# Reordering the first stage of a hybrid attention block: where the adaLN sums stand among the transposes of x

## The chip, the cores and the metric

One core of a Trainium2 chip runs the whole kernel. The metric is device time in microseconds, the median of several executions. The engines are TensorE (PE; its weight loads are listed apart as PEld), VectorE (DVE), ScalarE (ACT), GpSimd (POOL) and the queue of SyncE (SP), which issues all loads of this stage.

## The reference, cut to what matters

The block works on x (1024 tokens by 1024 channels, float32). The part that the change touches is its beginning:

```python
ada = c @ w_ada[l] + b_ada[l]
shift, scale, gate = jnp.split(ada, 3, axis=-1)
h = rms_norm(x, norm_w[l]) * (1.0 + scale[:, None, :]) + shift[:, None, :]
proj = h @ w_in[l]
(cq, ckv, k_rope, gate_a, q_b, k_b, v_b, f_b, gate_b, mg_a, mg_b) = jnp.split(proj, split_points, axis=-1)
```

After it come two attention branches, gates, and the output projection, in which this change does nothing.

## The kernel before, in words

x is cut into eight tiles of 128 rows (x0 to x7). `phase0` (from L246) turns them into h, channel by row, and multiplies h with the first columns of `w_in` (`w_cq`, 424 columns: the query latent, the rope key and the forget gate). Channels are cut into eight blocks of 128 (kt 0 to 7).

For each x tile ScalarE squares it and sums each row (`square`, L271; a second small instruction reads the sum). For each pair of tiles `scale` (L274 to L286) takes the root on ScalarE, polishes its reciprocal on VectorE in four small steps and multiplies both tiles (L286). TensorE transposes a scaled tile with eight transposes against the identity (`turn`, L136) into two PSUM banks, four channel blocks each. `evac` (L307 to L311) copies the two halves into `xT`. Before, ScalarE copies both.

For each channel block the adaLN shift and scale are a matrix product of c with a block of `w_ada` (two tiles of 512 KB). For blocks 0 and 1 TensorE does it (`ada_rows`, L313 to L320: two halves, shift and scale, of eight float32 matmuls, each of which the trace lists as two instructions). For blocks 2 to 7 VectorE does it in two sums of 128x1024 (`ada_cols`, L322 to L324) with `cb`, c in every row. `gain` (L326 to L329) makes of them the two columns `gs`.

Then h is split into a rounded part and a rest so that float32 accuracy comes out of three fast products: `high` (L335, ScalarE) writes the high part `hT_hi`, `modulate` (L340 on ScalarE or L342 on VectorE) overwrites `xT` with h, `low` (L347, VectorE) writes the difference `hT_lo`. `w_cq` is split in the same way (cast on ScalarE, difference on VectorE). `products` runs the three products of a channel block for a list of row tiles: part 0 is high by high, part 1 high by low weights, part 2 low by high; 24 matmuls for a block of all eight tiles.

The order is written out by hand: each engine executes its instructions in the order of the lines, and waits for the operands of the one at its head. Before, TensorE's order is 32 warm transposes of the identity, x0 and x1, x2 and x3, both halves of block 0's sums, x4 and x5, products of block 0 for rows 0 to 3, both halves of block 1's sums, x6, products for rows 4 and 5, x7, products of block 1 for rows 0 to 5, then both blocks for rows 6 and 7, then blocks 2 to 7. SP issues the loads in the order of the lines too; a load waits for the landing of the load eight places before it.

PSUM tags: `s` has two slots of two banks, `t` two of one, `o` and `f` one each. A tile of a tag waits until the readers of the slot's last tile are through. Later stages are interleaved by a planner (`fill_to`, L142) that counts TensorE's time in `pe_time`; a warm transpose adds 107 ns to it (L135). All its due times are set from `pe_time` itself, as in

```python
self.fill_to(self.pe_time + 600)
due = self.pe_time
```

Of the kernel before, what the change touches and what calls it, by code (L numbers as in the profile page):

```python
# [10 lines left out]
F32 = mybir.dt.float32  # L11
F32R = mybir.dt.float32r
# [3 lines left out]
ALU = mybir.AluOpType  # L16
# [3 lines left out]
P = 128  # L20
# [54 lines left out]
class Net:  # L75
# [78 lines left out]
    def consts(self):  # L154
        nc, t, U = self.nc, self.t, self.U
        cp = self.cp
        self.x0 = U.get([P, D], F32, "x0")
        nc.sync.dma_start(self.x0, t["x"][0:P, :])
        self.ident = cp.tile([P, P], F32, name="ident")
        nc.sync.dma_start(self.ident, t["ident"])  # L160
        self.vec = cp.tile([P, t["vec"].shape[1]], F32, name="vec")
        nc.sync.dma_start(self.vec, t["vec"])
        self.misc_raw = self.Hs.get([P, 512], F32, "misc")
        self.pos = cp.tile([P, ST], I32, name="pos")
        self.ones = cp.tile([P, 1], F32, name="ones")
        nc.gpsimd.memset(self.ones, 1.0)
        self.eps = cp.tile([P, 1], F32, name="eps")
        nc.gpsimd.memset(self.eps, EPS)
        v = self.vec
        self.c_col = v[:, 0:8]  # L170
        self.nw = v[:, 8:16]
        self.b_shift = v[:, 16:24]
        self.b_scale = v[:, 24:32]
        self.lq = v[:, 32:35]
        self.lkv = v[:, 35:37]
        self.vqa_raw = v[:, 37:38]
        self.vka = v[:, 38:39]
        self.vqb_raw = v[:, 39:40]
        self.vkb = v[:, 40:41]
        self.bf_row = v[:, 41:49]  # L180
        self.b_gate = v[:, 49:57]
        self.b1 = cp.tile([P, KT], F32, name="b1")
        nc.vector.tensor_scalar(out=self.b1, in0=self.b_scale, scalar1=1.0, scalar2=None, op0=ALU.add)
        self.vqa = cp.tile([P, 1], F32, name="vqa")
        nc.vector.tensor_scalar(out=self.vqa, in0=self.vqa_raw, scalar1=float(96.0 ** -0.5), scalar2=None, op0=ALU.mult)
        self.vqb = cp.tile([P, 1], F32, name="vqb")
        nc.vector.tensor_scalar(out=self.vqb, in0=self.vqb_raw, scalar1=0.125, scalar2=None, op0=ALU.mult)
        self.maskb = cp.tile([P, P], BF16, name="maskb")
# [52 lines left out]
    def phase0(self):  # L241
# [11 lines left out]
        def load_x(*sts):  # L253
            for st in sts:
                xs[st] = U.get([P, D], F32, f"x{st}")
                nc.sync.dma_start(xs[st], t["x"][st * P:(st + 1) * P, :])

        def load(kt):
            wada[kt] = [U.get([P, D], F32, f"wada{kt}{e}") for e in range(2)]
            for e in range(2):  # L260
                nc.sync.dma_start(wada[kt][e], t["w_ada"][kt][:, e])

        def load_cq(gi, half=None):
            if not half:
                cqw.append(U.get([P, 2, 424], F32, f"raw_cq{gi}"))
            k = slice(0, 2) if half is None else slice(half, half + 1)
            nc.sync.dma_start(cqw[gi][:, k], t["w_cq"][:, 2 * gi + k.start:2 * gi + k.stop])

        def square(st):
            junk = Hs.get([P, 512], F32, f"junk{st}")  # L270
            nc.scalar.activation(junk.bitcast(BF16), xs[st], AF.Square, accum_out=ssq[:, st:st + 1])  # L271
            Hs.put(junk)

        def scale(pair):  # L274

            a, b = pair
            v, y, q = (self.sp.tile([P, 32], F32, tag=f"rs_{n}", name=f"{n}_x{a}", bufs=2)[:, 0:2] for n in "vya")
            nc.vector.tensor_scalar(out=v, in0=ssq[:, a:b + 1], scalar1=1.0 / D, scalar2=EPS, op0=ALU.mult, op1=ALU.add)
            nc.scalar.activation(y, ssq[:, a:b + 1], AF.Sqrt, scale=1.0 / D, bias=self.eps)
            nc.vector.reciprocal(y, y)  # L280
            nc.vector.scalar_tensor_tensor(out=q, in0=y, scalar=-0.5, in1=y, op0=ALU.mult, op1=ALU.mult)
            nc.vector.tensor_tensor(out=q, in0=q, in1=v, op=ALU.mult)
            nc.vector.scalar_tensor_tensor(out=y, in0=q, scalar=1.5, in1=y, op0=ALU.add, op1=ALU.mult)
            r = y
            for i, st in enumerate(pair):
                nc.vector.tensor_scalar(out=xs[st], in0=xs[st], scalar1=r[:, i:i + 1], scalar2=None, op0=ALU.mult)  # L286

        def warm(n, src):

            for _ in range(n):  # L290
                self.transpose(self.warm_bank[:, 0:P], src[:, 0:P])
# [18 lines left out]
                src = pts[st][j].rearrange("p (k c) -> p k c", k=4)  # L310
                (nc.scalar.copy if e == "a" else nc.vector.tensor_copy)(xT[:, 4 * j:4 * j + 4, cols], src)  # L311

        def ada_rows(kt, bank):  # L313

            b = self.bank(bank, f"pada{kt}")
            for e in range(2):
                w = wada[kt][e].rearrange("p (r c) -> p r c", r=8)
                for rc in range(8):
                    self.mm(b[:, 64 * e:64 * e + 64], w[:, rc], col(rc).broadcast_to([P, 64]), rc == 0, rc == 7)
            return b[:, 0:1], b[:, 64:65]  # L320

        def ada_cols(kt, e):  # L322
            w, a = wada[kt][e], acc[:, kt, e:e + 1]
# [9 lines left out]
        def high(kt, sts=range(ST)):  # L333
            c = slice(sts[0] * P, (sts[-1] + 1) * P)
            nc.scalar.activation(hi[:, kt, c], xT[:, kt, c], AF.Identity, scale=gs[:, kt, 1:2], bias=gs[:, kt, 0:1])  # L335
# [23 lines left out]

        self.wg = {}  # L360
        self.gcol = self.sp.tile([P, 8], F32, name="gcol")
        load_x(1, 2, 3, 4, 5)
        load(0)
        load_x(6, 7)
        load_cq(0, 0)
        load(1)
        load_cq(0, 1)
        self.cb = U.get([P, D], F32, "cb")
        nc.sync.dma_start(self.cb, t["c_row"].broadcast_to([P, D]))
        load_cq(1)  # L370
        most, last = range(6), (6, 7)
        self.warm_bank = self.bank("f", "warm")
        root = self.sp.tile([P, 1], F32, name="root")
        nc.scalar.activation(root, self.eps, AF.Sqrt)
        for st in range(4):
            square(st)
            if st % 2:
                scale((st - 1, st))
        warm(32, self.ident)
        turn(0, "s")  # L380
        turn(1, "tt")
        evac(0)
        square(4)
        evac(1)
        square(5)
        scale((4, 5))
        turn(2, "s")
        turn(3, "tt")
        evac(2)
        rows = ada_rows(0, "o")  # L390
        evac(3)
        gain(0, rows)
        square(6)
        high(0, range(4))
        wh, wl = U.get([P, 2, 424], F32R, "hi_cq0"), U.get([P, 2, 424], F32R, "lo_cq0")
        nc.scalar.copy(wh[:, 0], cqw[0][:, 0])
        turn(4, "tt")
        turn(5, "of")
        load(2)
        load(3)  # L400
        modulate(0, range(4), "d")
        low(0, range(4))
        evac(4)
        square(7)
        scale((6, 7))
        nc.vector.tensor_tensor(out=wl[:, 0], in0=cqw[0][:, 0], in1=wh[:, 0].bitcast(F32), op=ALU.subtract)
        self.cqw.append((wh, wl))
        evac(5)
        high(0, (4, 5))
        accs = [self.bank("s", f"cq_s{i}") for i in range(2)]  # L410
        for st in range(4):
            banks[st] = accs[st // 2][:, st % 2 * 512:st % 2 * 512 + 512]
        products(0, range(4), (0, 2))
        rows = ada_rows(1, "t")
        modulate(0, (4, 5), "d")
        low(0, (4, 5))
        gain(1, rows)
        nc.scalar.copy(wh[:, 1], cqw[0][:, 1])
        products(0, range(4), (1, ))
        load_cq(2)  # L420
        load(4)
        nc.sync.dma_start(self.misc_raw[:, 0:t["misc"].shape[1]], t["misc"])
        nc.sync.dma_start(self.pos, t["pos"])
        turn(6, "tt")
        high(1, most)
        modulate(1, most, "d")
        evac(6)
        low(1, most)
        banks[4], banks[5] = self.bank("o", "cq_o"), self.bank("f", "cq_f")
        products(0, (4, 5))  # L430
        turn(7, "tt")
        evac(7)
        nc.vector.tensor_tensor(out=wl[:, 1], in0=cqw[0][:, 1], in1=wh[:, 1].bitcast(F32), op=ALU.subtract)
        U.put(cqw[0])
        products(1, most, (0, 2, 1))
        wh, wl = U.get([P, 2, 424], F32R, "hi_cq1"), U.get([P, 2, 424], F32R, "lo_cq1")
        ada_cols(2, 0)
        ada_cols(2, 1)
        gain(2)
        load(5)  # L440
        banks[6], banks[7] = self.bank("t", "cq_t0"), self.bank("t", "cq_t1")
        for kt in range(2):
            high(kt, last)
            modulate(kt, last, "a")
        nc.scalar.copy(wh, cqw[1])
        for kt in range(2):
            low(kt, last)
        for kt in range(2):
            products(kt, last)
        high(2)  # L450
        modulate(2, engine="a")
        nc.vector.tensor_tensor(out=wl, in0=cqw[1], in1=wh.bitcast(F32), op=ALU.subtract)
# [995 lines left out]
def layout(i):  # L1448
# [21 lines left out]
    vec[0:64, 40] = vec[64:, 40] = a["kn_b"][0]  # L1470
    vec[:, 41:49] = a["b_f"][0][None, :]
    vec[:, 49:57] = b[2048:].reshape(8, P).T
    o["vec"] = vec
    o["c_row"] = np.ascontiguousarray(a["c"][0].reshape(1, D))
    o["pos"] = np.ascontiguousarray(a["positions"][0].reshape(8, P).T)
    inv = np.power(np.float32(10000), -np.arange(0, 32, 2, dtype=f) / np.float32(32)).astype(f)
# [3 lines left out]
    misc[:, 48:80] = a["kn_rope_a"][0]  # L1480
    misc[:, 80:208] = np.where(np.tril(np.ones((P, P), bool)), f(0), f(NEG))
    o["misc"] = misc
    o["ident"] = np.eye(P, dtype=f)
    r = np.arange(64)
    o["tri"] = ((r[:, None] // 8 == r[None, :] // 8) & (r[:, None] % 8 < r[None, :] % 8)).astype(f)
    o["w_cq"] = _chunks(np.concatenate([w_in[:, 0:384], w_in[:, 640:672], w_in[:, 2720:2728]], 1), 8)
# [31 lines left out]
```

## Time and profile before

| | us |
|---|---|
| median of 3 runs | 962.1 (961.2 to 963.23) |
| profiled execution, its own time | 961.75 |
| its span, first to last instruction | 959.9 |
| TensorE busy in the span | 947.9 (99%) |
| VectorE busy | 633.2 (66%) |
| ScalarE busy | 477.3 (50%) |
| GpSimd busy | 208.1 (22%) |

Times in the rows are microseconds from the start of the span, unless ns is said. The stage in question is the first 63 us. L numbers are lines of the kernel; L127 and L136 are the helpers through which all matmuls and transposes go, so there the tile names tell the groups apart.

### The profile page before, as it was taken

Reading aid. Unit: us, or ns where it says so; the run is one execution under the profiler, and the core shown is the slowest. Engines: PE = TensorE matmul, PEld = TensorE weight load, DVE = VectorE, ACT = ScalarE, POOL = GpSimd, SP = SyncE. Lnnn points to the kernel's source line nnn. Section 1 sums busy time; section 2 is a strip of 40 time slices with the busy share of each in tenths; the row PEclk is TensorE's granted clock in tenths of the full one; section 3 lists DMA queues with packets and bytes.
Section 4 is the critical chain, followed back from the end, with each engine's and each line's share of the span. In section 5 each row is a group of like instructions: output and inputs, shape, how many; then the busy total and the mean of one; then the engine's idle time right before and its main releaser. Section 6 shows DMA issues by size and latency. Waiting matters only on the chain.

```text
span 959.9 us, 14942 instructions
## 1 busy us (share of the span) xinstructions
PE 947.9 (99%) x5390; PEld 820.6 (85%) x5390; DVE 633.2 (66%) x1379; ACT 477.3 (50%) x959; POOL 208.1 (22%) x260
## 2 busy tenths in 40 slices
PE   7999999999999999999999999999999999999998
PEld 7999999998878888888888888888888888888887
DVE  3977877778366667657667676667676766495222
ACT  7776624543245556556555566465565654143000
POOL 0022142200012222221233333232333220046000
PEclk9999999999999999999999999999999999999999
DMA  9831132951973225235332232222421554644321
GB/s 340 334 98 45 51 114 62 323 216 40 343 232 110 88 67 132 71 95 133 99 91 68 66 101 89 80 88 89 120 70 46 186 186 154 238 147 138 103 88 66
DMA packets 79961, 124.96 MB, mean 130 GB/s; under 512 B 5928, under 2 KB 47536, under 8 KB 79888
## 3 DMA queue, kind: packets, MB, share of 16 engines
q1 hardware_dynamic: 79888, 124.01, 39.4%
q8 instruction: 42, 0.69, 0.3%
q14 instruction: 31, 0.25, 0.1%
HBM read 88.33 MB, written 35.66 MB: 129 GB/s over the span
## 4 chain that ended last, share of the span: by engine, by line
PE 92%; DMA 3%; DVE 2%; ACT 2%; issue 1%; SPq 1%; POOL 0%; ACTq 0%; DVEq 0%; POOLq 0%
PE f L127 36%; PE out L127 9%; PE s L127 9%; PE b L127 8%; PE o L127 7%; PE pt L136 6%; PE q L127 3%; PE ckv L127 2%; PE kv L127 2%; PE cq_s L127 2%; PE bv L127 1%; PE cq_t L127 1%; DMA x_u<-in_x 1%; PE pada L127 1%; DMA va_d<-vhl_u 1%
## 5 line engine op out<-in xcount | busy, mean ns | idle before, releaser
L1207 ACT CAST pp_u<-pt 128x512 fp32r<-128x512 f32 x192 | 91.9, 479 | 171.1 <-PE pt L136 155.0
L1208 DVE TENSOR_TENSOR pp_u<-pt,pp_u 128x512 fp32r<-128x512 f32 x192 | 106.7, 556 | 84.8 <-ACT pp_u L1207 81.9
L127 PE MATMUL f<-hT_lo,hi_f_u 128*128 128x512 f32 x384 | 153.6, 400 | 0.0
L127 PE MATMUL f<-hT_hi,lo_f_u 128*128 128x512 f32 x384 | 153.4, 399 | 0.0
L127 PE MATMUL f<-hT_hi,hi_f_u 128*128 128x512 f32 x384 | 153.1, 399 | 0.0
L127 PE MATMUL s<-k_u,q_u 96*128 96x512 f32 (+6 forms) x480 | 116.8, 362 | 0.9 <-DMA k_u<-kr_d 0.9
L1181 DVE TENSOR_REDUCE nm<-s 128x1 f32<-128x128 f32 (+7 forms) x128 | 97.0, 758 | 4.4
L1191 POOL TENSOR_SCALAR p_u<-p_u,rs 128x640 f32<-128x640 f32 (+1 forms) x64 | 64.3, 1004 | 164.1 <-DVE rs L1190 119.0
L1191 POOL TENSOR_SCALAR p_h<-p_h,rs 128x128 f32<-128x128 f32 (+1 forms) x64 | 41.7, 652 | 247.3 <-DVE rs L1190 208.2
L127 PE MATMUL o<-pp_u,v_u 128*128 128x512 f32 (+7 forms) x384 | 94.2, 340 | 0.0
L127 PEld LDWEIGHTS s<-k_u,q_u 96*128 96x128 f32 (+2 forms) x480 | 77.0, 190 | 7.3 <-issue 0.9
L127 PEld LDWEIGHTS f<-hT_hi,hi_f_u 128*128 128x128 f32 x384 | 72.4, 189 | 12.1
L127 PEld LDWEIGHTS f<-hT_hi,lo_f_u 128*128 128x128 f32 x384 | 72.4, 189 | 11.2
L127 PEld LDWEIGHTS f<-hT_lo,hi_f_u 128*128 128x128 f32 x384 | 72.5, 189 | 11.1
L127 PEld LDWEIGHTS o<-pp_u,v_u 128*128 128x128 f32 (+1 forms) x384 | 61.8, 161 | 19.5
L127 PE MATMUL b<-hi_b_u,hT_hi 128*128 128x256 f32 x256 | 73.1, 285 | 0.0
L127 PE MATMUL b<-hi_b_u,hT_lo 128*128 128x256 f32 x256 | 72.4, 283 | 0.0
L127 PE MATMUL b<-lo_b_u,hT_hi 128*128 128x256 f32 x256 | 72.4, 283 | 0.0
L136 PEld LDWEIGHTS pt<-ident,p_u 128*128 128x128 f32 x416 | 52.7, 140 | 16.7
L136 PE MATMUL pt<-ident,p_u 128*128 128x128 f32 x416 | 66.2, 272 | 0.0
L1187 ACT ACTIVATE p_u<-s,nm 128x640 f32<-128x640 f32 (+1 forms) x64 | 61.5, 961 | 4.3 <-DVE nm L1181 3.2
L127 PE MATMUL out<-lo_wo_u,hT_hi 128*128 128x512 f32 (+1 forms) x136 | 51.2, 377 | 0.0
(318 smaller groups left out, 2073.1 us busy)
## 6 DMA issues: line engine op xcount, KB each, us to landing
raw_f_u<-in_w_t SPq DMA_DIRECT2D x24, 512.0 KB
wada_u<-in_w_ada SPq DMA_DIRECT2D x16, 512.0 KB
mg_d<-th_h SPq DMA_DIRECT2D x32, 256.0 KB
mg_h<-mg_d SPq DMA_DIRECT2D x32, 256.0 KB
x_u<-in_x SPq DMA_DIRECT2D x8, 512.0 KB
raw_b_u<-in_w_b SPq DMA_DIRECT2D x8, 512.0 KB
raw_wg_u<-in_w_gate SPq DMA_DIRECT2D x8, 512.0 KB
va_d<-vhl_u SPq DMA_DIRECT2D x8, 512.0 KB
```

What stands on the lines that cost most here:

```text
L127: self.nc.tensor.matmul(out, lhsT=l, rhs=r, start=start, stop=stop)
L136: self.nc.tensor.transpose(out=out, in_=in_, identity=self.ident)
L1181: nc.vector.tensor_reduce(out=nm, in_=sv, axis=AX.X, op=ALU.max, negate=True)
L1187: nc.scalar.activation(p[:, 0:w], sv, AF.Exp, bias=nm, accum_out=sm)
L1191: nc.gpsimd.tensor_scalar(out=p[:, 0:w], in0=p[:, 0:w], scalar1=rs, scalar2=0.0, op0=ALU.mult, op1=ALU.add)
L1207: nc.scalar.copy(ph[:, c0:], pt[:, c0:])
L1208: nc.vector.tensor_tensor(out=pl[:, c0:], in0=pt[:, c0:], in1=ph[:, c0:].bitcast(F32), op=ALU.subtract)
```

## The change

Identity and constant vectors become one tensor with one load. The loads' order becomes x0, constants, x1, block 0 of `w_ada`, x2, x3, block 1, x4, x5, the first half block of `w_cq`, x6, x7, the second half block. `ada_rows` becomes `ada_row`, one half of a block's sum at a time. Evacuations are "ad": ScalarE copies channel blocks 0 to 3 of a tile, VectorE 4 to 7. TensorE's order becomes 24 warm transposes, the first half sum of block 0, x0, x1, its second half, x2, x3, both halves of block 1, products of block 0 for rows 0 to 3, x4, x5, products of block 1 for rows 0 to 3, x6, x7, products of both blocks for rows 4 to 7, then blocks 2 to 7 as before.

```diff
-        self.ident = cp.tile([P, P], F32, name="ident")
-        nc.sync.dma_start(self.ident, t["ident"])
-        self.vec = cp.tile([P, t["vec"].shape[1]], F32, name="vec")
-        nc.sync.dma_start(self.vec, t["vec"])
+        both = cp.tile([P, t["vec"].shape[1]], F32, name="vec")
+        nc.sync.dma_start(both, t["vec"])
+        self.ident, self.vec = both[:, 0:P], both[:, P:]
...
+        def ada_row(kt, e, bank):
+
+            w = wada[kt][e].rearrange("p (r c) -> p r c", r=8)
+            for rc in range(8):
+                self.mm(bank[:, 64 * e:64 * e + 64], w[:, rc], col(rc).broadcast_to([P, 64]), rc == 0, rc == 7)
+            return bank[:, 64 * e:64 * e + 1]
...
-        load_x(1, 2, 3, 4, 5)
+        load_x(1)
         load(0)
+        load_x(2, 3)
+        load(1)
+        load_x(4, 5)
+        load_cq(0, 0)
         load_x(6, 7)
-        load_cq(0, 0)
-        load(1)
         load_cq(0, 1)
...
+        front, rest = range(4), range(4, 8)
+        square(0)
+        square(1)
+        scale((0, 1))
+        warm(24, self.ident)
+        bank = self.bank("o", "pada0")
+        a0 = ada_row(0, 0, bank)
         turn(0, "s")
         turn(1, "tt")
+        a1 = ada_row(0, 1, bank)
+        evac(0, "ad")
+        square(2)
+        evac(1, "ad")
+        square(3)
+        gain(0, (a0, a1))
+        scale((2, 3))
+        high(0, (0, 1))
+        wh, wl = U.get([P, 2, 424], F32R, "hi_cq0"), U.get([P, 2, 424], F32R, "lo_cq0")
+        modulate(0, (0, 1), "d")
+        low(0, (0, 1))
+        turn(2, "s")
+        turn(3, "tt")
+        bank = self.bank("f", "pada1")
+        rows = [ada_row(1, e, bank) for e in range(2)]
         square(4)
+        evac(2, "ad")
+        evac(3, "ad")
+        high(0, (2, 3))
+        nc.scalar.copy(wh[:, 0], cqw[0][:, 0])
+        modulate(0, (2, 3), "d")
+        low(0, (2, 3))
+        nc.vector.tensor_tensor(out=wl[:, 0], in0=cqw[0][:, 0], in1=wh[:, 0].bitcast(F32), op=ALU.subtract)
+        self.cqw.append((wh, wl))
+        load(2)
         square(5)
         scale((4, 5))
...
-        products(0, range(4), (0, 2))
-        rows = ada_rows(1, "t")
-        modulate(0, (4, 5), "d")
-        low(0, (4, 5))
+        products(0, front, (0, 2, 1))
         gain(1, rows)
+        high(1, front)
+        modulate(1, front, "d")
+        low(1, front)
+        turn(4, "tt")
+        turn(5, "of")
+        load(3)
         nc.scalar.copy(wh[:, 1], cqw[0][:, 1])
-        products(0, range(4), (1, ))
+        evac(4, "ad")
+        nc.vector.tensor_tensor(out=wl[:, 1], in0=cqw[0][:, 1], in1=wh[:, 1].bitcast(F32), op=ALU.subtract)
+        U.put(cqw[0])
+        square(6)
+        evac(5, "ad")
+        square(7)
+        scale((6, 7))
+        products(1, front, (0, 2, 1))
...
         turn(6, "tt")
+        turn(7, "of")
+        ada_cols(2, 0)
+        evac(6, "ad")
+        evac(7, "ad")
+        wh, wl = U.get([P, 2, 424], F32R, "hi_cq1"), U.get([P, 2, 424], F32R, "lo_cq1")
+        high(0, rest)
+        modulate(0, rest, "a")
+        ada_cols(2, 1)
+        low(0, rest)
+        gain(2)
+        high(1, rest)
+        modulate(1, rest, "a")
+        low(1, rest)
+        load(5)
...
         nc.scalar.copy(wh, cqw[1])
         for kt in range(2):
-            low(kt, last)
-        for kt in range(2):
-            products(kt, last)
+            products(kt, rest, (0, 2, 1))
```

## Rows read from the trace of the kernel before

**Rows 1.** The page: busy time of the engines, and the chain by engine.
```profile
PE 947.9 (99%) x5390; PEld 820.6 (85%) x5390; DVE 633.2 (66%) x1379; ACT 477.3 (50%) x959; POOL 208.1 (22%) x260
...
PE 92%; DMA 3%; DVE 2%; ACT 2%; issue 1%; SPq 1%; POOL 0%; ACTq 0%; DVEq 0%; POOLq 0%
```

**Rows 2.** TensorE's waits, whole span: total, times, longest (us).
```profile
PE warm L136 <- DMA ident<-in_ident: 4.6, 1, 4.6
PE xt L136 <- DVE x_u L286: 1.0, 1, 1.0
PE bv L127 <- DVE lo_b_u L116: 1.0, 1, 1.0
```

**Rows 3.** Timeline of the weight loads: start, us, what, [idle before <-releaser].
```profile
10.38 1.73 PEld L136 LDWEIGHTS xt<-ident,x_u 128*128 128x128 f32 x16
13.37 0.85 PEld L136 LDWEIGHTS xt<-ident,x_u 128*128 128x128 f32 x8 [1.26 <-DVE x_u L286]
14.41 0.90 PEld L136 LDWEIGHTS xt<-ident,x_u 128*128 128x128 f32 x8 [0.19 <-ACT xT L311]
15.29 3.65 PEld L127 LDWEIGHTS pada<-vec,wada_u 128*128 128x128 f32 x32
18.80 1.79 PEld L136 LDWEIGHTS xt<-ident,x_u 128*128 128x128 f32 x16
20.86 0.69 PEld L127 LDWEIGHTS cq_s<-hi_cq_u,hT_hi 128*128 128x128 f32 x4 [0.27 <-ACT hi_cq_u L396]
21.73 0.68 PEld L127 LDWEIGHTS cq_s<-hi_cq_u,hT_lo 128*128 128x128 f32 x4 [0.19 <-DVE hT_lo L347]
```

**Rows 4.** Timeline of TensorE: first product of block 2, first of the next stage.
```profile
35.56 0.93 PE L127 MATMUL cq_s<-hi_cq_u,hT_hi 128*128 128x424 f32 x4
...
63.16 0.28 PE L127 MATMUL ckv<-hi_ckv_u,hT_hi 128*128 128x256 f32 x1
```

**Rows 5.** Windows, warm transposes alone: us, PE busy (count), PEclk, DMA share, GB/s.
```profile
4.62:9.15 4.53, 4.53 (x21) 1.00 0.96 370
9.15:10.40 1.25, 1.25 (x12) 1.00 1.02 419
```

**Rows 6.** Timeline of ScalarE.
```profile
9.01 1.06 ACT L271 ACTIVATE junk_h<-x_u 128x1024 bf16<-128x1024 f32 x1 [0.26 <-DMA x_u<-in_x]
9.97 0.19 ACT L271 ACTIVATION_READ_ACCUMULATOR junk_h<-x_u 128x1 f32 x1
...
15.93 0.29 ACT L279 ACTIVATE y_x<-xssq,eps 128x2 f32<-128x2 f32 x1
16.13 2.03 ACT L311 COPY xT<-xt 128x512 f32<-128x512 f32 x4
...
19.56 0.81 ACT L335 ACTIVATE hT_hi<-xT,gs 128x512 fp32r<-128x512 f32 x1 [0.36 <-DVE gs L329]
20.28 0.53 ACT L396 CAST hi_cq_u<-raw_cq_u 128x424 fp32r<-128x424 f32 x1
```

**Rows 7.** The chain, start to 12 us: start, us, what (ends as x3 lands).
```profile
3.07 7.17 DMA x_u<-in_x
```

**Rows 8.** Timeline of VectorE.
```profile
16.25 0.17 DVE L280 RECIPROCAL y_x<-y_x 128x2 f32<-128x2 f32 x1 [0.16 <-ACT y_x L279]
...
17.04 1.42 DVE L286 TENSOR_SCALAR x_u<-x_u,y_x 128x1024 f32<-128x1024 f32 x2
...
19.12 0.22 DVE L328 TENSOR_SCALAR gs<-pada,vec 128x1 f32<-128x1 f32 x1 [0.66 <-PE pada L127]
...
20.41 0.55 DVE L342 TENSOR_SCALAR xT<-xT,gs 128x512 f32<-128x512 f32 x1 [0.94 <-ACT hT_hi L335]
20.98 0.69 DVE L347 TENSOR_TENSOR hT_lo<-xT,hT_hi 128x512 fp32r<-128x512 f32 x1
...
30.14 1.22 DVE L324 SCALAR_TENSOR_TENSOR wada_u<-wada_u,cb_u 128x1024 f32<-128x1024 f32 x1
```

**Rows 9.** Groups of VectorE by form, whole span: busy us, mean ns, idle before.
```profile
L1208 DVE TENSOR_TENSOR pp_u<-pt,pp_u 128x512 fp32r<-128x512 f32 x96 | 66.1, 689 | 37.4 <-ACT pp_u L1207 36.2
```

More of the change, by code (lines that the diff above doesn't have):

```diff
@@ L311, in evac @@
                 (nc.scalar.copy if e == "a" else nc.vector.tensor_copy)(xT[:, 4 * j:4 * j + 4, cols], src)
[L313 to L320, printed above, removed]
+        def ada_row(kt, e, bank):
[3 more added lines that the diff above has]
+            return bank[:, 64 * e:64 * e + 1]
         def ada_cols(kt, e):
@@ L370, in phase0 @@
         load_cq(1)
-        most, last = range(6), (6, 7)
         self.warm_bank = self.bank("f", "warm")
@@ L374, in phase0 @@
         nc.scalar.activation(root, self.eps, AF.Sqrt)
[L375 to L379, printed above, removed]
+        front, rest = range(4), range(4, 8)
[5 more added lines that the diff above has]
+        a0 = ada_row(0, 0, bank)
         turn(0, "s")
         turn(1, "tt")
-        evac(0)
-        square(4)
-        evac(1)
+        a1 = ada_row(0, 1, bank)
[13 more added lines that the diff above has]
+        rows = [ada_row(1, e, bank) for e in range(2)]
+        square(4)
+        evac(2, "ad")
[7 more added lines that the diff above has]
+        load(2)
         square(5)
         scale((4, 5))
[L387 to L409, printed above, removed]
         accs = [self.bank("s", f"cq_s{i}") for i in range(2)]
@@ L424, in phase0 @@
         turn(6, "tt")
[L425 to L428, printed above, removed]
-        banks[4], banks[5] = self.bank("o", "cq_o"), self.bank("f", "cq_f")
[L430 to L440, printed above, removed]
+        turn(7, "of")
[12 more added lines that the diff above has]
+        load(5)
+        banks[4], banks[5] = self.bank("o", "cq_o"), self.bank("f", "cq_f")
         banks[6], banks[7] = self.bank("t", "cq_t0"), self.bank("t", "cq_t1")
-        for kt in range(2):
-            high(kt, last)
-            modulate(kt, last, "a")
         nc.scalar.copy(wh, cqw[1])
         for kt in range(2):
-            low(kt, last)
-        for kt in range(2):
-            products(kt, last)
+            products(kt, rest, (0, 2, 1))
         high(2)
@@ L1472, in layout @@
     vec[:, 49:57] = b[2048:].reshape(8, P).T
-    o["vec"] = vec
+    o["vec"] = np.concatenate([np.eye(P, dtype=f), vec], 1)
     o["c_row"] = np.ascontiguousarray(a["c"][0].reshape(1, D))
@@ L1482, in layout @@
     o["misc"] = misc
-    o["ident"] = np.eye(P, dtype=f)
     r = np.arange(64)
```

## The prediction

> **What bounds the kernel now.** I read the page first, then TensorE's waits, then the first 65 us by engine. TensorE is busy 99% of the span and makes up 92% of the chain that ended last [rows 1]. Its waits in the whole run are few: 4.6 us for the identity at the start, then 1.0 us for the scaling of an x tile; none is longer [rows 2]. So a change in the first stage is worth what it does to the time at which TensorE leaves that stage; everything later follows it. In the weight-load timeline the real work starts at 10.38 (transposes of x0), once x0 is scaled, and its gaps from there on are 1.26, 0.19, 0.27 and 0.19, together 1.9 us [rows 3]. The stage's six last blocks start at 35.56, the next stage (ckv) at 63.16, with 24 products a block and 0.19 us a product, gapless [rows 4]. So the most that can be won is 1.9 us of gaps and what can be started before 10.38.
>
> The profiled execution took 961.75 us (span 959.9, 1.85 around it), 0.35 under the median of 962.1. I sum against 961.75 and add 0.35 at the end. A measurement can tell about 0.2%, 1.9 us, from no change.
>
> **Start and warm-up.** TensorE's 21 first warm transposes took 4.53 us, 0.216 each (the 1.2 GHz level), the 12 after 9.15 took 0.104 each (2.4 GHz), though the granted clock reads 1.00 in both [rows 5]. The rise came in a run of nothing but transposes. With 24 of them instead of 32 TensorE is through at 9.15 + 3 x 0.11 = 9.5, at the high level. The Trainium skill, "TensorE: Matmul & The Clock Gate", Part 4, says that transposes do not count as busy time that lifts the clock. The trace disagrees here; what it would do to the sums is rival (5).
>
> **Loads.** SP issues one load less (identity and vector become one); POOL has none. Blocks 0 of w_ada take the places that x2 and x3 had, which landed at 9.01 [rows 6] and 10.24 [rows 7], so at 9.0 and 10.2. One 512 KB place is worth 1.25 us by these two, so x2 and x3 land near 11.5 and 12.8, x4 and x5 (four places later) near 16.5 and 17.8, x6 and x7 near 20 and 21.5. The first half block of w_cq has the same bytes ahead of it as before, when its cast ran at 20.28 [rows 6]. Below, each square starts after its tile's landing for another reason, except x4's, whose wait hides nothing. So the loads' order costs nothing by itself. The merged load gives between 0 and 0.4 us of landing (one issue of SP); nothing waits on that, I take 0.
>
> **Sums and transposes on TensorE, to x2.** One sum of 32 instructions took 18.80 - 15.29 = 3.5 us, 16 transposes 1.74 (10.38 plus 1.73) [rows 3]. The first half sum runs from 9.5 to 11.3, x0 and x1 are turned by 13.0, the second half sum ends at 14.8. That is a start 0.9 us earlier than 10.38. Next in TensorE's order are the transposes of x2. ScalarE must first copy its half of x0 (0.48 us each: four in 2.03) from 11.9, square x2 (1.06) to 13.45, copy its half of x1 to 13.9, square x3, whose sum is read 1.15 after its start, at 15.1, and take the root (0.29) to 15.4 [rows 6]. The reciprocal on VectorE to the first scaled tile takes 16.25 to 17.8, 1.55 us [rows 8]: x2 is ready at 17.0. VectorE's gain waits for the second half sum until 15.0 and is queued ahead of this scaling; it is through as the root ends, so costs nothing. **TensorE waits from 14.8 to 17.0, 2.3 us**, where it waited 1.26.
>
> **To x6.** Then TensorE does 1.74 of transposes, 3.5 of sums (to 22.3), 12 products (2.3, to 24.6), x4 and x5 (to 26.3) and 12 products (to 28.6). Their operands are in time: the cast of the first weights ends near 20.1; x4 and x5, squared by 21.1, are scaled at 23.0 and 23.7. But on VectorE gain 1 stands behind these scalings and ends at 24.0 though its sums were there at 22.5, and ScalarE, done at 21.4, waits for it 2.6 us with the high part of block 1 (L335) at the head of its queue. Behind that stand the second cast, two copies and the squares of x6 and x7: 24.0 + 0.72 + 0.45 + 0.5 + 1.06 + 0.48 + 1.15 = 28.4, root 28.7, x6 scaled at 30.3. **TensorE waits from 28.6 to 30.3, 1.7 us.** It covered this before with other work.
>
> **After x7.** The transposes of x6 and x7 end at 32.1. In the new order TensorE has then nothing but products of these rows. VectorE's half copies stand behind a column sum of block 2 (1.22 us, L324) [rows 8] that starts at 30.9, so they end at 33.3. ScalarE's high part ends at 33.2. **Wait 1.2 us.** After four products the low part is wanted at 34.1; ScalarE's modulated copy ends at 34.0, but the second column sum holds VectorE until 34.4 and the low part takes 0.69: 35.1. **Wait 1.0 us.** A VectorE copy from PSUM of 128x512 is not in the trace: between 0.55 (same width from SBUF, L342 in [rows 8]) and 0.69 (a two-operand one that reads PSUM [rows 9]); I take 0.66, nearer the row that reads PSUM. The ends move the sum by 0.2.
>
> **Sum.** New waits 2.3 + 1.7 + 1.2 + 1.0 = 6.2; old gaps gone, -1.9; earlier start, -0.9: +3.4 us. The halved evacuations take eight copies (3.8 us) from ScalarE, which shortens its chains as used above; in the second of them ScalarE spends the gift waiting. From block 2 on VectorE is late by 2.7 us against TensorE's 3.4 (it starts its w_cq split at 36.4 where it was 33.8), so no new wait arises. The planner of the later stages counts eight transposes less, but all its due times are set relative to its own count, so the later order stays. 961.75 + 3.4 + 0.35 = **965.5**.
>
> Bounds of the unknowns: landings 0.3 earlier to 0.5 later, -0.3 to +0.2; copies -0.2 to +0.1; if ScalarE's high parts wait for VectorE's half of the tile too (by region they need only its own), +1.3. That is 965.0 to 967.1.
>
> **Rivals.** (1) *The queues run ahead*: the waits on x2 and x6 do not arise, because ScalarE, with half the copies, reaches the squares in time. It decides at 14.8 and 28.6. Then +2.2 - 1.9 - 0.9 = -0.6, 961.5: no change. For it: eight copies fewer. Against: the squares stand behind copies that wait for TensorE. With only one of the two waits it lies between, 963 to 964. (2) *Faster*: besides, TensorE is not held after x7, because VectorE gets its copies and low part done before the column sums matter; all four waits are gone, 961.5 - 2.2 = 959.3. It takes x7 evacuated as the last transpose ends, against the 1.22 us sum queued ahead. (3) *The clock falls* in the thin stretch from 28.6 to 35, where TensorE works 2.5 of 6.5 us. The price is a second slow start: 21 transposes in 4.53 us that take 2.3 at 0.109, so 2.2 us: 967.7. For it: before, no gap after 10.38 is over 1.26 [rows 3], so the trace has not tried one; against: the single gaps are at most 2.3. The same page of the Trainium skill, in its section on why this matters, asks for no long idle between bursts of matmuls; no run here shows what it takes. (4) *The change does not do what it says*: the blocks land late, since loads in flight share the engines, and the first half sum starts at 10.2 (x3's old place) rather than 9.5: +0.7 passed on, 966.2, inside the forecast. (5) *The first half sum runs at the low level*, because the rise comes later or because transposes alone do not bring it: 16 instructions at twice 0.11, 1.8 us more ahead of all that follows, 967.3. For it: the rise came only 0.35 before the point at which the sums now start; against: the rows after 9.15 [rows 5].
>
> **Chances.** Forecast with its bounds and (4) 0.66; clock (3) 0.10; slow first sum (5) 0.04; no change (1) 0.13; faster (2) 0.07. So slower by over 0.2% (above 964.0) 0.80, within 0.2% 0.13, faster 0.07. The range must reach above 967.7 for (3) with its spread and down into the partly hidden cases of (1): 962.8 to 968.2; it leaves out (2) and the lower part of (1).
>
> **What would show it.** Right: the first pada group at about 9.5; the x2 transposes idle about 2 us on VectorE's scaling (L286), and the x6 ones again about 1.7 near 30; gaps before the products of the last four tiles; ScalarE idle some 2.6 us on gs before its high part of 128x512; the ckv group near 66.5 instead of 63.16. Wrong: the ckv group at or before 63, or x6's transposes without idle time (then (1) or (2)); the transposes near 31 at 0.2 us each (then (3)); the w_ada sums waiting on a load (then (4)).

## The result, and the profile after

The changed kernel takes 969.96 us (median of 5 executions, 967.19 to 972.65) where the kernel before took 962.2 beside it (961.2 to 964.13): ratio 1.0076, interval [1.0048, 1.0104]. The forecast was 965.5 and its range ended at 968.2. The profiled execution is the fastest of the five: 967.19, span 965.4, mean granted clock 0.998. The other four have clocks of 0.992 to 0.998.

The page of the changed kernel, busy time and chain, against [rows 1]:

```profile
PE 948.9 (98%) x5382; PEld 820.9 (85%) x5382; DVE 638.5 (66%) x1387; ACT 474.1 (49%) x951; POOL 208.3 (22%) x260
...
PE 90%; DMA 2%; DVE 2%; issue 2%; ACT 2%; SPq 1%; POOL 1%; POOLq 0%; DVEq 0%; ACTq 0%
```

Eight warm transposes are gone and eight copies have moved from ScalarE to VectorE. TensorE is busy 1.0 us longer in a span that is 5.5 us longer, although the eight transposes, some 0.8 us of work by the pace in [rows 5], are gone: most of the loss is idle time, and some 1.8 us is slower work. TensorE's waits from 4 to 48 us (total, times, longest; against [rows 2]):

```profile
PE warm L136 <- DMA vec<-in_vec: 4.7, 1, 4.7
PE xt L136 <- DVE x_u L285: 4.2, 2, 2.5
PE cq_o L127 <- ACT hT_hi L332: 1.1, 1, 1.1
PE cq_o L127 <- DVE hT_lo L344: 0.6, 1, 0.6
```

The wait on a scaled tile was 1.0 us once; it is now 4.2 us in two places, and two waits before the products of the last row tiles are new. The weight-load timeline gives their places (start, us, what, idle before and what ended it; against [rows 3]):

```profile
9.44 1.86 PEld L127 LDWEIGHTS pada<-vec,wada_u 128*128 128x128 f32 x16 [0.20 <-DMA wada_u<-in_w_ada]
...
17.47 1.73 PEld L136 LDWEIGHTS xt<-vec,x_u 128*128 128x128 f32 x16 [2.68 <-DVE x_u L285]
...
30.97 1.73 PEld L136 LDWEIGHTS xt<-vec,x_u 128*128 128x128 f32 x16 [1.99 <-issue]
...
34.02 0.19 PEld L127 LDWEIGHTS cq_o<-hi_cq_u,hT_hi 128*128 128x128 f32 x1 [1.32 <-ACT hT_hi L332]
...
35.66 0.19 PEld L127 LDWEIGHTS cq_o<-hi_cq_u,hT_lo 128*128 128x128 f32 x1 [0.95 <-DVE hT_lo L344]
```

Four gaps, 2.68 + 1.99 + 1.32 + 0.95 = 6.94 us, where before they came to 1.9. The second is marked "issue", but the view of the waits has two waits on x_u, so it is the wait for x6. ScalarE's timeline of the same kernel (against [rows 6]) shows who is late for whom:

```profile
12.36 0.59 ACT L310 COPY xT<-xt 128x512 f32<-128x512 f32 x1 [4.37 <-PE xt L136]
12.84 1.06 ACT L270 ACTIVATE junk_h<-x_u 128x1024 bf16<-128x1024 f32 x1
...
15.55 0.29 ACT L278 ACTIVATE y_x<-xssq,eps 128x2 f32<-128x2 f32 x1
...
24.65 0.82 ACT L332 ACTIVATE hT_hi<-xT,gs 128x512 fp32r<-128x512 f32 x1 [2.53 <-DVE gs L326]
...
28.98 0.30 ACT L278 ACTIVATE y_x<-xssq,eps 128x2 f32<-128x2 f32 x1
...
33.16 0.81 ACT L332 ACTIVATE hT_hi<-xT,gs 128x512 fp32r<-128x512 f32 x1
```

The squares of x2 and x3 begin at 12.84, behind the copy at 12.36 that waited for TensorE's transposes, and the root follows at 15.55. ScalarE then stands 2.53 us idle before the high part at 24.65, with the squares of x6 and x7 behind it; their root comes at 28.98. VectorE's timeline (against [rows 8]) has the other side:

```profile
16.66 1.42 DVE L285 TENSOR_SCALAR x_u<-x_u,y_x 128x1024 f32<-128x1024 f32 x2
...
24.40 0.21 DVE L326 SCALAR_TENSOR_TENSOR gs<-pada,b,vec 128x1 f32<-128x1 f32 x1
...
26.69 0.69 DVE L310 COPY xT<-xt 128x512 f32<-128x512 f32 x1
...
33.78 1.22 DVE L321 SCALAR_TENSOR_TENSOR wada_u<-wada_u,cb_u 128x1024 f32<-128x1024 f32 x1
34.92 0.08 DVE L321 DVE_READ_ACCUMULATOR wada_u<-wada_u,cb_u 128x1 f32 x1
34.92 0.69 DVE L344 TENSOR_TENSOR hT_lo<-xT,hT_hi 128x512 fp32r<-128x512 f32 x1
```

The copy from PSUM, bounded by 0.55 and 0.69 before, takes 0.69 [rows 9]. The column sum at 33.78 does end right before the low part that the last wait is for.

What the forecast did not have stands in the windows of TensorE (us, busy and count, PEclk, DMA share, GB/s; against [rows 5]):

```profile
34.00:36.00 2.00, 1.39 (x6) 1.00 1.02 393
36.00:38.00 2.00, 2.00 (x8) 0.51 1.03 407
38.00:40.00 2.00, 2.00 (x8) 0.63 1.02 404
40.00:42.00 2.00, 2.00 (x12) 1.00 1.04 416
```

Behind the last two waits the granted clock falls from 1.00 to 0.5 (2.4 to 1.2 GHz) and stays there from about 36.0 to 39.5. In that stretch TensorE is busy all the time, but its rows count 8 products in 2 us instead of 12. The next stage then starts (TensorE's timeline; 63.16 in [rows 4]):

```profile
68.77 0.28 PE L127 MATMUL ckv<-hi_ckv_u,hT_hi 128*128 128x256 f32 x1
```

That is 5.6 us later, and the span is 5.5 us longer: in this execution the whole loss lies in the first stage.

### The profile page after: what moved, and what is told of

Read it like the earlier page. It is cut to its first block, busy times and chain, and to the rows that moved or that the text cites. A ratio compares the mean times of both kernels' runs of the same rounds, so it can differ in the third digit from the quotient of the medians.

```text
span 965.4 us, 14923 instructions
## 1 busy us (share of the span) xinstructions
PE 948.9 (98%) x5382; PEld 820.9 (85%) x5382; DVE 638.5 (66%) x1387; ACT 474.1 (49%) x951; POOL 208.3 (22%) x260
## 4 chain that ended last, share of the span: by engine, by line
PE 90%; DMA 2%; DVE 2%; issue 2%; ACT 2%; SPq 1%; POOL 1%; POOLq 0%; DVEq 0%; ACTq 0%
PE f L127 36%; PE out L127 9%; PE s L127 9%; PE b L127 8%; PE o L127 7%; PE pt L136 6%; PE q L127 3%; PE kv L127 2%; PE ckv L127 2%; PE cq_s L127 1%; PE bv L127 1%; PE cq_t L127 1%; DMA va_d<-vhl_u 1%; DMA q_u<-qr_d 1%; PE kt L136 1%
## 5 line engine op out<-in xcount | busy, mean ns | idle before, releaser
L136 PEld LDWEIGHTS pt<-vec,p_u 128*128 128x128 f32 x416 | 52.7, 140 | 16.7
L136 PE MATMUL pt<-vec,p_u 128*128 128x128 f32 x416 | 66.2, 272 | 0.0
```

The lines of the kernel that those rows point to most:

```text
L136: self.nc.tensor.transpose(out=out, in_=in_, identity=self.ident)
```

## The experiments

Twelve kernels ran, in three groups of four; each group had the kernel before on the same chip. Because most of the differences turned out to hang on the clock, each execution's time is also taken apart: us lost to the clock = (1 - mean granted clock) x span. The rest is called the time at full clock. The clock is given to 0.001, about 1 us, so only means over many executions are used. The lost part is an upper bound, since a low clock costs nothing while TensorE waits or is through. In the trace of the kernel before, all of the 0.9 us that it counts lies behind TensorE's last product (its windows):

```profile
947.00:956.20 9.20, 9.19 (x64) 1.00 0.20 71
...
958.00:959.93 1.93, 0.00 (x0) 0.54 0.19 64
```

This end counts for 0.1 to 0.9 us in the traces of the old order and for 0 to 0.5 in those of the new one, so a difference of half a microsecond in the lost part says little. The row "before" holds the 80 executions of the three groups (one of 3355 us is left out), "after" the 5 of the result and the 5 of the first experiment.

```
kernel         n   median   ratio [95%]               mean us = at full clock + lost
before         80                                     963.6     962.5           1.1
after          10           see text                  971.4     966.7           4.7
fill_x2        11  968.72   1.0052 [1.0034, 1.0070]   968.6     967.3           1.3
fill_late       7  971.52   1.0074 [1.0047, 1.0100]   970.7     966.2           4.4
fill_all        8  967.70   1.0045 [1.0026, 1.0064]   967.7     966.7           1.0
ahead67        12  969.59   1.0070 [1.0046, 1.0094]   970.7     965.3           5.4
ahead67_fill   10  967.89   1.0049 [1.0031, 1.0068]   968.4     966.5           1.8
after_aa        6  975.16   1.0112 [1.0092, 1.0133]   974.5     968.5           6.0
one_load       12  963.46   0.9995 [0.9978, 1.0011]   963.6     962.2           1.4
shared         12  962.66   0.9998 [0.9980, 1.0016]   963.9     962.8           1.1
before_look    12  964.77   1.0001 [0.9983, 1.0018]   964.1     962.6           1.5
gap_x2         12  965.75   1.0023 [1.0008, 1.0037]   966.0     964.1           1.9
gap_x2_fill    12  964.11   1.0004 [0.9993, 1.0015]   963.8     963.8           0.0
```

Two theories stood against each other on the loss: that the four waits are the whole loss, and that the low clock behind them is a large part of it, so that TensorE kept busy with idle transposes in the waits would win time back without shortening any wait.

**after_again**, the changed kernel once more.

> The changed kernel as it is, for a second look. Theory (four waits of TensorE plus a clock that falls in the thin stretch, by chance of its phase): the waits come back within 0.3 us (2.7 before x2, 2.0 before x6, 1.3 and 0.9 after x7), at least one stretch of about 3.4 us at clock 0.5 between 15 and 45 us, time 967 to 973, and slower executions have a lower mean clock. Rival (the spread comes from a later stage): executions of the same mean clock differ by several us, and the next stage's first group stays at 68.8.

It took 971.98 (969.58 to 977.9), ratio 1.0095 [1.0068, 1.0122]. Its trace has the same four waits (2.68, 1.96, 1.32, 0.95), but the low clock comes at another place. TensorE's windows of this kernel:

```profile
17.00:18.00 1.00, 0.45 (x4) 1.00 1.04 395
18.00:20.00 2.00, 2.00 (x14) 0.62 1.03 402
20.00:22.00 2.00, 2.00 (x12) 0.53 1.04 397
22.00:24.00 2.00, 2.00 (x20) 1.00 1.03 394
```

Here the fall follows the wait before x2, and the same two waits after x7 bring none. In both traces the low level lasts 3.4 us and the next stage starts 5.6 to 5.8 late (68.77 and 68.94). A second fall stands far behind the stage, at the start of the attention (same view, later windows):

```profile
279.00:283.00 4.00, 0.73 (x3) 1.00 1.01 321
283.00:285.00 2.00, 1.75 (x8) 0.93 0.96 311
285.00:288.00 3.00, 3.00 (x10) 0.50 0.43 145
```

TensorE waits there 3.2 us for k_u to be read back for the attention. That wait is in every trace of either order, from 0.2 us (shared) to 3.2, and is one reason why executions of one kernel differ. It does not always bring a fall: 2.1 us in one_load and 2.9 in gap_x2 bring none.

**fill_x2, fill_late, fill_all**: idle transposes of the identity in the waits.

```diff
+        warm(22, self.ident)                                # fill_x2, fill_all
         turn(2, "s")
...
+        warm(16, self.ident, self.bank("t", "fill"))        # fill_late, fill_all
         turn(6, "tt")
...
+        warm(10, self.ident, banks[6])                      # fill_late, fill_all
         nc.scalar.copy(wh, cqw[1])
```

> 22 idle transposes of the identity (2.4 us) put into the wait before x2 only. The wait itself stays, so no wait is shortened. Theory: if the idle time before x2 causes some of the clock's falls, the median goes down by 1 to 3 us and the late stretch still falls in some executions (965.5 to 969). If only the late stretch matters: 967 to 973 as before.

> 16 idle transposes before those of x6 (1.7 us) and 10 before the products of the last four row tiles (1.1 us); both waits stay as long as they were. Theory: no fall in the stretch from 29 to 45 us, the next stage starts near 67.1 instead of 68.8, time 965 to 967; if falls before x2 matter too, some executions stay above 967.

> Both fillings together. Theory: clock 1.00 throughout after the warm-up in every execution, only the four waits are left of the loss: next stage near 67.1, time 965.0 to 966.5, spread under 2 us. Rival (the clock is not the cause of the rest): median stays at 968 to 971.

With all waits filled no fall is left in the trace, the next stage starts at 67.14, and the clock costs 1.0 us a run, as before the change (1.1). The time at full clock stays at 966.7: the idle transposes shorten nothing, they only keep the clock. Without the formula it comes out the same: the 52 executions of the kernel before with a clock of 0.999 or 1.000 take 962.5 us in the mean, the five such of fill_all 966.6, 4.1 more. The forecast of a spread under 2 us failed: the eight executions of fill_all lie within 5.4 us, and three of them read 0.998. TensorE's timeline and windows of fill_all:

```profile
67.14 0.28 PE L127 MATMUL ckv<-hi_ckv_u,hT_hi 128*128 128x256 f32 x1
```

```profile
14.00:18.00 4.00, 3.86 (x35) 1.00 1.03 402
28.00:36.00 8.00, 7.41 (x55) 1.00 1.04 394
36.00:40.00 4.00, 4.00 (x23) 1.00 1.02 404
```

Filling the wait before x2 alone takes 3.4 of the 4.7 us away (standard error of the difference about 1.0, from the spread of the executions); filling the later ones alone takes next to nothing. The trace of fill_x2 has no fall in the first stage at all, though its later waits (1.97, 1.32, 0.95) stand as they were; the next stage starts at 67.76, 0.6 behind fill_all, and x2's transposes are as late already (18.03 instead of 17.41). In the profiled execution of fill_late the low level behind the wait before x2 lasts 13.7 us. TensorE's windows of fill_late:

```profile
14.00:18.00 4.00, 1.56 (x14) 0.92 1.03 404
18.00:22.00 4.00, 3.89 (x19) 0.50 1.03 398
22.00:26.00 4.00, 4.00 (x21) 0.50 1.03 403
26.00:31.00 5.00, 5.00 (x20) 0.50 1.03 404
31.00:36.00 5.00, 5.00 (x35) 1.00 1.04 390
```

TensorE is busy in all of it but the first 0.7 us, with transposes, float32 sums and products. The next stage starts at 73.96, 6.8 us behind fill_all: half of 13.7.

**ahead67**: the squares and scaling of x6 and x7 ahead of what waits for gain 1.

```diff
         products(0, front, (0, 2, 1))
+        square(6)
+        square(7)
         gain(1, rows)
+        scale((6, 7))
         high(1, front)
...
-        square(6)
         evac(5, "ad")
-        square(7)
-        scale((6, 7))
```

> The changed kernel with the squares of x6 and x7 ahead of block 1's high part in ScalarE's order and their scaling ahead of its modulation in VectorE's. Theory (ScalarE's idle 2.5 us behind gain 1 makes x6 late): the wait before x6's transposes (2.0 us) goes to under 0.3; about 1 us of it comes back as waits of the products of block 1 on VectorE; the next stage starts 1 to 1.5 us earlier than in the changed kernel at equal clock (67.1 without a fall), and the thin stretch is fuller, so the late fall gets rarer: median 1 to 3 us under the changed kernel. Rival (x6 is late for its landing): the wait stays at 2 us.

**ahead67_fill**: the same, and 22 idle transposes before x2.

> The changed kernel with the squares and scaling of x6 and x7 ahead, and 22 idle transposes in the wait before x2. Theory: no fall in the first stage, next stage at 65.6 to 66.0 (67.4 with a fall before), waits before x2 2.7 (filled), after x7 1.3 and 0.9; median 965 to 966.5, 2.5 to 3 us over before. Rival (the thin stretch after x7 still falls): executions at 0.995 and less remain.

The wait before x6 is gone in both traces (0.35 us remains in the first, 0.71 + 0.43 in the second, before products), so the queue named in the forecast was the cause: at full clock ahead67 is 1.4 us below the changed kernel (standard error 0.6). The filled kernel is only 0.2 below it, but by the next stage's start, less half of the low stretch, the two are at 65.7 and 66.0 where fill_all is at 67.14. But the wait before x2 still costs the clock, 5.4 us; filled, 1.8. The trace of ahead67_fill shows that the thin stretch after x7 can bring the fall by itself, with waits of 1.32 and 0.89 only; so its median lies above the forecast of 965 to 966.5, as the rival had it. TensorE's windows:

```profile
30.00:35.00 5.00, 3.38 (x23) 1.00 1.03 392
35.00:36.00 1.00, 1.00 (x6) 0.67 1.04 399
36.00:38.00 2.00, 2.00 (x7) 0.50 1.02 404
38.00:39.00 1.00, 1.00 (x5) 0.63 1.08 418
```

**one_load**: the kernel before, with the merged constants and 24 warm transposes.

```diff
-        nc.sync.dma_start(self.ident, t["ident"])
...
-        nc.sync.dma_start(self.vec, t["vec"])
+        both = cp.tile([P, t["vec"].shape[1]], F32, name="vec")
+        nc.sync.dma_start(both, t["vec"])
...
-        warm(32, self.ident)
+        warm(24, self.ident)
```

> The kernel before with identity and constants in one load and 24 warm transposes, nothing else. Theory: x1 lands near 6.5 instead of 7.3, x0's transposes start near 9.6 instead of 10.4; x2 and x3 land within 0.5 us of before, so the wait before x2 grows by what is won: next stage 62.5 to 63.6 (63.2 before), time within 0.1% of before. Rival: all of the start's 0.8 us is kept (62.4).

The next stage starts at 62.63, 0.5 us earlier. ScalarE's timeline has the reason, the squares of x1 and x2:

```profile
7.00 1.06 ACT L270 ACTIVATE junk_h<-x_u 128x1024 bf16<-128x1024 f32 x1 [1.36 <-DMA x_u<-in_x]
...
8.38 1.04 ACT L270 ACTIVATE junk_h<-x_u 128x1024 bf16<-128x1024 f32 x1
```

Before, x2's square began at 9.01 [rows 6] and x1's at 7.28 (ScalarE's timeline of the kernel before):

```profile
7.28 1.06 ACT L271 ACTIVATE junk_h<-x_u 128x1024 bf16<-128x1024 f32 x1 [1.69 <-DMA x_u<-in_x]
```

The eight warm transposes that are gone may have a part in it: in the kernel before the last of them end at about 10.4 [rows 5], just where x0's transposes start (10.38, [rows 3]); here these start at 10.10. No run parts them from the load. In the time of the whole kernel half a microsecond is not seen: ratio 0.9995 [0.9978, 1.0011].

**shared**: the kernel before with all evacuations "ad".

```diff
-        def evac(st, engines="aa"):
+        def evac(st, engines="ad"):
```

> The kernel before with evacuations shared between ScalarE and VectorE, nothing else. Theory: VectorE, which is nearly full from 30 to 58 us, starts block 2's column sums later and TensorE meets waits on low parts: next stage 0.5 to 1.5 us later (63.7 to 64.7). Rival (ScalarE is what holds the stage): 0.3 to 1 us earlier.

**after_aa**: the changed kernel with all evacuations on ScalarE, at all eight calls.

```diff
-        evac(0, "ad")
+        evac(0, "aa")
```

> The changed kernel with all evacuations on ScalarE again, the rest of the change kept. By the order of the queues the wait before x2 grows by about 1 us, that before x6 by about 1.4, the one after x7 by 0.4: next stage 2 to 3 us later than in the changed kernel at equal clock (69 to 70 without a fall), more falls. So sharing wins some 2.5 us inside this order. Rival (sharing costs, as in the kernel before): earlier.

The edit has opposite signs in the traces of the two orders. In the old one TensorE now waits for a copy of VectorE's (0.56 us) and for low parts (0.35 and 0.40). The next stage starts at 64.32, 1.2 later, of which 0.5 is there before the first copy (x0's transposes start at 10.85 instead of 10.38); the whole time shows no difference (0.9998). In the new order the two squares behind ScalarE's copies set the waits, and taking the sharing back lengthens every one but the last (weight-load timeline of after_aa):

```profile
18.98 3.27 PEld L136 LDWEIGHTS xt<-vec,x_u 128*128 128x128 f32 x16 [3.65 <-DVE x_u L285]
35.87 1.73 PEld L136 LDWEIGHTS xt<-vec,x_u 128*128 128x128 f32 x16 [2.94 <-issue]
39.37 0.19 PEld L127 LDWEIGHTS cq_o<-hi_cq_u,hT_hi 128*128 128x128 f32 x1 [1.78 <-ACT hT_hi L332]
40.95 0.22 PEld L127 LDWEIGHTS cq_o<-hi_cq_u,hT_lo 128*128 128x128 f32 x1 [0.90 <-DVE hT_lo L344]
```

9.27 us of waits instead of 6.94, 1.8 more at full clock, and 6.0 lost to the clock. Its trace has two falls in the first stage (windows of TensorE):

```profile
17.00:24.00 7.00, 5.02 (x24) 0.51 1.04 399
41.00:44.50 3.50, 3.50 (x10) 0.51 0.69 275
```

They last 6.8 and 3.4 us. The first begins some 1.8 us before the wait on x2 ends at 18.98, so up to 0.9 of its loss is counted while TensorE waits.

**before_look**, the kernel before with nothing changed.

> The kernel before as it is, for a second look at where its own spread (961 to 967) comes from. Theory: the first stage is as before (63.2, no fall of the clock), and executions above 963 have a wait of more than 1.5 us on k_u near 274 us, some with a fall after it. Rival: falls in the first stage here too.

Neither its trace nor any other of the old order has a fall between the rise and TensorE's last product. Its executions fall into two groups: at a clock of 0.999 or 1.000 they take 961.1 to 962.1, at 0.996 or 0.998 they take 964.6 to 966.6. So the kernel before pays for the clock too, in some executions, 1 to 1.5 us on average by the formula. The profiled execution is one of the short ones, so whether the longer ones have the forecast wait on k_u stays open.

**gap_x2**: the kernel before with idle VectorE work that delays x2. **gap_x2_fill**: the same, with 22 idle transposes in that wait.

```diff
+            if st == 3:
+                late = U.get([P, D], F32, "late")
+                nc.vector.tensor_scalar(out=late, in0=xs[3], scalar1=1.0, scalar2=None, op0=ALU.mult)
...
+        warm(22, self.ident)                                # gap_x2_fill
         turn(2, "s")
```

> The kernel before with four idle VectorE instructions (2.8 us) ahead of the scaling of x2 and x3, nothing else of the change. The wait before x2 grows from 1.3 to about 2.8 us. Theory (a wait of this length there lets the clock fall behind it in many executions): next stage at 64.7 without a fall, 66.4 with one of 3.4 us, more with a longer one; some executions with a mean clock of 0.995 or less, median 1.5 us above the sum of wait and before (964 to 968). Rival (the wait costs its length alone): every execution with the mean clocks of before, median +1.5 us.

> The same, with 22 idle transposes (2.4 us) in the wait. Theory: no fall in the first stage, next stage at 64.7, no execution with a mean clock under 0.996, median about 1.5 us over before. Rival (the wait's length is all): the same median as gap_x2.

The wait before x2 is made as long as in the changed kernel (weight-load timeline of gap_x2):

```profile
15.35 1.73 PEld L136 LDWEIGHTS xt<-ident,x_u 128*128 128x128 f32 x16 [2.68 <-DVE x_u L286]
```

Its trace shows no fall in the first stage, and over 12 executions the clock costs 1.9 us, 0.8 more than before. At full clock it is 1.6 slower, which the longer wait explains (2.68 - 1.26 = 1.4). Filled, all 12 executions have a clock of 1.000 and lie within 2.3 us of each other. It is the one kernel here that lost nothing to the clock, at the attention's start included. So filling this wait takes 1.9 us (standard error 0.5) of clock off gap_x2, and 3.4 (1.0) off the changed kernel: that the same wait costs less in the old order is not shown clear of noise.

## Why the prediction was wrong

**The direction and the waits were right.** The table of steps, in us:

```
step                                  forecast   after's trace
wait before x2                          2.3        2.68
wait before x6                          1.7        1.99
waits after x7                          1.2, 1.0   1.32, 0.95
old gaps gone                          -1.9       -1.9
first sum at 9.5 instead of 10.38      -0.9       -0.94
sum                                    +3.4       +4.1
```

At full clock the loss is 966.7 - 962.5 = 4.2 us by the executions' means, and 67.14 - 63.16 = 4.0 by the next stage's start in fill_all. The largest miss among the terms is the 0.4 us on x2 (2.3 was 17.0 - 14.8, rounded up): the root came at 15.55 instead of 15.1. ScalarE's idle time on gs, 2.6 by forecast and 2.53 by the trace, is the queue that was named; ahead67 shows it by removing it. The column sum ahead of the last low part stood where it was put, but ScalarE's modulated copy (L337, 34.01 for 0.82 us) ends at 34.8, so the sum's end at 34.92 is not shown to be the sole cause of that wait, and no run took the sum away.

**The step that failed** is rival (3), "the clock falls in the thin stretch from 28.6 to 35", with a price of 2.2 and a chance of 0.10, set aside with "the single gaps are at most 2.3". Three things were wrong in it. It is no rare case: all five traces of this order in which the wait before x2 is not filled (after, after_again, fill_late, ahead67, after_aa) have a fall in the first stage, in four of them in or right behind that wait; of the three in which it is filled, ahead67_fill alone has one, behind its later waits. It looked at the wrong wait: the one before x2 brings most of the falls, since filling it takes 3.4 us off the changed kernel and 3.6 off ahead67. And the price is not fixed: 1.7 us for a low stretch of 3.4 (the work of half the time), four times that for the 13.7 of fill_late, and after_aa has two stretches. On average the change pays 4.7 - 1.1 = 3.6 us (standard error 0.9) for the clock, almost as much as for its waits; 4.2 + 3.6 = 7.8, the loss of the result. Not all of it belongs to the first stage: the two traces of the changed kernel lose 1.7 us each there, and the second as much again at the attention's start.

The argument against the rival was read from too little: before, no gap was over 1.26 and none brought a fall, which says nothing on one of 2.3. The Trainium skill ("TensorE: Matmul & The Clock Gate", the section on why this matters) asks for no long idle between bursts of matmuls. The runs agree in so far as filling the idle time wins clock back: 3.4 us in the changed kernel. How long is too long they do not settle: 2.68 us before x2 came with a fall in after_again and fill_late, and with none there in the first trace of the changed kernel and in gap_x2's.

**Rival (1) and (2)**, the queues that run ahead, did not happen: both waits came. **Rival (4)**: the first sum started at 9.44 with 0.20 us of waiting for its load, in three other traces of this order at 9.29 to 9.57 after 0.41 to 0.92; late by a few tenths only. In the other four (9.38 to 9.75) it followed the warm transposes without a wait. **Rival (5)** did not happen in the trace of the result: of the 24 warm transposes 19 took 4.01 us from 4.69 on, 0.211 each, and the last ones, to 9.4, 0.1 each, so the clock was up before the sums, after nothing but transposes. In fill_x2 and fill_late it came later, in small: their 24 warm transposes took 4.98 us, 0.207 each, the first sum began at 9.75 and 9.60 still at that pace, and x2's transposes began 0.6 us later than in fill_all and in the result's trace.

**The merged load** was taken at nothing; one_load shows 0.5 us of the first stage, for the load and the eight warm transposes together. In the changed kernel x1's earlier landing sets nothing, since there the first sum goes first and waits for its own load; whether that load lands sooner for the merging no run shows. **Sharing the copies** was rightly costed as a help inside the new order (after_aa).

**What stays open.** Why the same 2.68 us brings a fall in some executions and none in others was not settled, nor whether it costs more in the changed order than in gap_x2 (3.4 against 1.9 us by filling it, with errors of 1.0 and 0.5); what TensorE does before it differs (24 warm transposes and sums against 32 warm transposes), and no run separated that. The two waits after x7 were never taken away, so their cause rests on the forecast and the timelines. Nor is it settled whether the change bears on the later fall at the attention's start: it stands in five of the eight traces of the new order and in none of the six of the old one, yet fill_all, with the new order, loses no more to the clock than the kernel before. No kernel here beats the kernel before by more than a measurement can tell.

## What to carry to other kernels

On an engine with a clock that falls, a new wait has two prices: its length, and the slow stretch that can follow it. When a change brings a wait longer than any in the trace, give the second price a large chance, put it on the longest wait, and test it by filling the wait with idle transposes, which changes the clock and not the waits. Split executions by their granted clock before comparing: here executions of the same changed kernel lay 8 us apart (969.58 at 0.998, 977.9 at 0.990).

## What the runs showed that was not expected

- Idle transposes of the identity hold TensorE's clock: with 22 of them in a wait of 2.68 us the mean clock was 1.000 in 12 of 12 executions (gap_x2_fill), without them between 0.994 and 1.000 (gap_x2).
- A low stretch can go on while TensorE is busy: 13.7 us in fill_late, nearly all of it busy. The others last 3.4 us, but for 6.8 in after_aa's first and in ahead67 and ahead67_fill at the attention's start.
- Where a fall comes differs between executions of one kernel: behind the wait before x2 (18.5) in after_again, behind the waits after x7 (36.0) in the first trace of the same kernel.
- The read-back of k_u that the attention starts with keeps TensorE waiting 0.4 us in one execution and 3.2 in another of the same kernel, and a fall can follow that too.
